# Low parts of the first attention's probabilities folded into idle rows of the outer key chunks

## The chip, the cores and the metric

The kernel runs on one core of one Trainium2 chip. A core has a matrix engine (TensorE, PE in the profile, with its weight loads shown apart as PEld), a vector engine (VectorE, DVE), a scalar engine (ScalarE, ACT), a general engine (GpSimd, POOL) and a queue-only engine (SyncE, SP) that here issues almost all DMA transfers. Each engine runs its instructions in a fixed order. The metric is the time of one execution on the device in microseconds (us); the median of several runs is compared.

## The reference: one encoder layer with two attentions

The reference computes one layer over 2048 tokens of width 1024: a norm, one wide input product, two attentions, a gated merge, and an MLP of width 4096 with a final norm. Only the first attention matters here:

```python
def windowed_gqa(q, k, v, sink):          # q (B,S,8,64); k,v (B,S,2,64)
    ...
    def block(i):                         # 128 queries, 384 keys from (i-1)*128
        ...
        dist = jnp.abs(q_pos[:, None] - k_pos[None, :])
        valid = (dist <= A_WINDOW) & (k_pos[None, :] >= 0) & (k_pos[None, :] < s)
        sc = jnp.einsum('bqkgd,bskd->bkgqs', qi, ki).astype(jnp.float32) * scale
        sc = sc - slopes[:, :, None, None] * dist.astype(jnp.float32)
        sc = jnp.where(valid, sc, -jnp.inf)
        ...
        p = jax.nn.softmax(jnp.concatenate([sc, sink_col], axis=-1), axis=-1)[..., :-1]
        return jnp.einsum('bkgqs,bskd->bqkgd', p.astype(v.dtype), vi)
```

There are 16 blocks of 128 queries, 2 key/value groups of 4 query heads each, head size 64, and a window of 128 tokens to each side (A_WINDOW). All of it is float32.

## The kernel before: one attention unit and what runs around it

Products keep float32 accuracy by splitting each operand in a rounded high part and the low rest. [...] Helpers `split` (L296, L297) and `mm3`/`mm3s` (L203 to L205, L300 to L302) do this all over the kernel.

The first attention is cut into 32 units, `attn_a(g, i)`: group g, query block i. Its first half (up to `yield`, L798) loads the queries with four transfers into `q` (L774, tag "qa", 3 buffers) and makes the scores. The 128 queries of 4 heads are regrouped in four sub-blocks u of 32 queries by 4 heads, so a sub-block fills 128 rows. Sub-block u looks at 288 keys only, from 32u to 32u+288 of the 384 that belong to the block (L780). Two matmuls make the scores of a sub-block (L785), DVE adds the bias and takes the maximum (L787), ACT takes the exponentials (L789 to L792), DVE sums and inverts (L793, L794), POOL scales (L796). The tile `s` (tag "sa") is 128 rows by 4 sub-blocks by 384 keys, and its columns outside the 288 keys were zeroed once (L754) and stay zero.

Its second half multiplies the probabilities by v. For each chunk c of 128 keys (three of them; the first block has no chunk 0, the last no chunk 2, so there are 92 chunks in all, and 60 of them are outer ones, c = 0 or 2), PE turns four 128x128 pieces into `pt` (L803): 128 keys in the rows, 512 columns in the order (u, head, query). ACT rounds `pt` to the high part `ph` (L806), DVE subtracts to get the low part `pl` (L807), and PE multiplies both by the same weights, v's 128 rows for this chunk with the high parts of v in columns 0 to 63 and the low parts in columns 64 to 127 (L808 for `ph`, L809 for `pl`). ACT and DVE add the two halves of the result `po` (L814, L815) and a transfer stores it (`y_a`, issued at L176).

In an outer chunk many rows of `pt` are zero. In chunk 0, sub-block u starts at key 32u, so for u = 2 and 3 (columns 256 to 511) rows 0 to 63 are zero. In chunk 2, sub-block u ends before row 32(u+1), so for u = 0 and 1 (columns 0 to 255) rows 64 to 127 are zero.

The first halves run two units ahead of the second halves (`drive`, L829). The weights of v come from `va` (L762), which `load_kv` fills per group and per half of the sequence. Between the attention's instructions lie those of the rest of the input product for the last two token blocks ("filler": `qk_tile`, `v_tile`, `gate_tile`, 24 matmuls of 128x512 for one tile, PE lines L203 to L205), which `paced` (L839) ties to the end of earlier units through `issue_after(done[at])`, where `done` holds each unit's last matmul. All loads of queries, keys, v and filler weights and the stores of results are issued by SP in one queue, in order.

The order on each engine, and on SP's queue, is not the order of the code: a planner (`TileContext(nc, schedule_with_timeline_sim=True)`) simulates the program with its own costs and writes down the order that its simulation gives. A tile of a ring with 3 buffers waits, in the plan and by a semaphore on the chip, until the last reader of the tile three back is done. Any change to the instructions may thus change the planned order of others.

Of the kernel before, what the change touches and what calls it, by code (L numbers as in the profile page):

```python
# [8 lines left out]
F32 = mybir.dt.float32  # L9
F32R = mybir.dt.float32r  # L10
AF = mybir.ActivationFunctionType
ALU = mybir.AluOpType
# [10 lines left out]
P = 128  # L23
# [72 lines left out]
def encoder_layer(ctx, tc, x, norm_mix, w_in, b_gate, sink, rpb, w_pa, w_pb, w_out,  # L96
                  norm_mlp, w_up, w_down, norm_final, dist_a, mask_b, out):
    nc = tc.nc
    V, A, G, PE, SY = nc.vector, nc.scalar, nc.gpsimd, nc.tensor, nc.sync

    def pool(name, side=None, space=None, stack=None):
        kw = {"reuse_waits": "tile"} if space is not DRAM else {}
        if side:
            kw["side"] = side
        if space:
            kw["space"] = space
        return (stack or ctx).enter_context(tc.tile_pool(name=name, bufs=1, **kw))

    def pools(stack, side, tags, name):

        return {t: pool(f"{name}_{t}", side=side, stack=stack) for t in tags}
# [9 lines left out]
    def psum(tag, bufs):  # L121
        n_ps[0] += 1
        return pps[tag].tile([P, 512], F32, tag=tag, bufs=bufs, name=f"{tag}_{n_ps[0]}")
# [3 lines left out]
    def T(pl, shape, dt, tag, bufs):  # L127
        n_t[0] += 1
        pl = pl[tag] if isinstance(pl, dict) else pl
        return pl.tile(shape, dt, tag=tag, bufs=bufs, name=f"{tag}_{n_t[0]}")  # L130
# [25 lines left out]
    vs_a = [dp.tile([2, P, 8, P], F32, name=f"vs_a{m}") for m in range(2)]  # L156
# [14 lines left out]
    def put(dst, src):  # L171
        pending.append((dst, src))

    def flush(keep=0, queue=A):
        while len(pending) > keep:
            queue.dma_start(*pending.pop(0))  # L176
# [398 lines left out]
    for p in range(2):  # L575
        t = T(xp, [P, D], F32, "xin", 8).rearrange("p (k c) -> p k c", k=4)
        c = QUADS[2][0]
# [93 lines left out]
    s_h = ExitStack()  # L671
    hpl = [pool(f"hT{n}", side="left", stack=s_h) for n in range(4)]
    s_a = ExitStack()
    ap_ = pools(s_a, "left", ("ka1", "va1", "qa", "sta", "sa", "ya", "dist", "ph", "pl", "biasa1", "byhead"), "a")
    ap_.update(pools(s_a, "right", ("biasa0", "va0", "ka0"), "a"))
    hp = {}

# [49 lines left out]
    dist = T(ap_, [P, A_K], F32, "dist", 1)  # L727
# [5 lines left out]
    for h in range(4):  # L733
        at = slice(h * A_Q, (h + 1) * A_Q)
# [4 lines left out]
    def make_bias_a(g):  # L739
        t = T(ap_, [P, A_K], F32, f"biasa{g}", 1)  # L740
        G.tensor_scalar(t, dist, slope[:, g : g + 1], 1.0, ALU.mult, ALU.mult)
        bias_a[g] = t
# [21 lines left out]
    def attn_a(g, i):  # L764
        c0, c1 = (1 if i == 0 else 0), (2 if i == 15 else 3)
        if bias_a[g] is None:

            with tc.issue_after(shares[2]):
                make_bias_a(g)
        base = (i - 1) * P  # L770
        q = T(ap_, [P, 4, 4, A_Q], F32R, "qa", 3)
        s = sas[len(began) % 4]
        for h in range(4):
            asked = SY.dma_start(q[:, :, h].bitcast(F32), qs_a[g][i // 8][:, h, i % 8].rearrange("p (u q) -> p u q", u=4)).ins  # L774
        began.append(asked)
        ka, v = kas[g], vas[g]
        st = T(ap_, [P, 8, 4], F32, "sta", 8)
        mx, nm, sm, es, ri = (st[:, k, :] for k in range(5))
        sink_g = sink_p[:, g : g + 1]
        span = [(max(u * A_Q, c0 * P), min(u * A_Q + A_K, c1 * P)) for u in range(4)]  # L780
        for u, (lo, hi) in enumerate(span):
            n = hi - lo
            ps = psum("s", 3)
            for z in range(2):
                PE.matmul(ps[:, :n], q[:, u].rearrange("p h q -> p (h q)"), ka[:, z, base + lo : base + hi],  # L785
                          start=z == 0, stop=z == 1)
            V.tensor_tensor_reduce(out=s[:, u, lo:hi], in0=ps[:, :n], in1=bias_a[g][:, lo - u * A_Q : hi - u * A_Q],  # L787
                                   scale=1.0, scalar=sink_g, op0=ALU.add, op1=ALU.max, accum_out=mx[:, u : u + 1])
        A.activation(nm, mx, AF.Copy, scale=-1.0)  # L789
        A.activation(es, mx, AF.Exp, bias=sink_g, scale=-1.0)  # L790
        for u, (lo, hi) in enumerate(span):
            A.activation(s[:, u, lo:hi], s[:, u, lo:hi], AF.Exp, bias=nm[:, u : u + 1], accum_out=sm[:, u : u + 1])  # L792
        V.tensor_tensor(out=sm, in0=sm, in1=es, op=ALU.add)  # L793
        V.reciprocal(ri, sm)  # L794
        for u, (lo, hi) in enumerate(span):
            share = G.tensor_scalar(s[:, u, lo:hi], s[:, u, lo:hi], ri[:, u : u + 1], 1.0, ALU.mult, ALU.mult)  # L796
        shares.append(share.ins)
        yield  # L798
        po = psum("av", 1)
        for c in range(c0, c1):  # L800
            pt = psum("pt", 2)
            for u in range(4):
                PE.transpose(pt[:, u * P : (u + 1) * P], s[:, u, c * P : (c + 1) * P], ident)  # L803
            ph = T(ap_, [P, 512], F32R, "ph", 3)
            pl = T(ap_, [P, 512], F32R, "pl", 3)
            A.copy(ph, pt)  # L806
            V.tensor_tensor(out=pl, in0=pt, in1=ph.bitcast(F32), op=ALU.subtract)  # L807
            PE.matmul(po, v[:, i - 1 + c, :], ph, start=c == c0, stop=False)  # L808
            last = PE.matmul(po, v[:, i - 1 + c, :], pl, start=False, stop=c == c1 - 1).ins  # L809
        done.append(last)  # L810
        t = T(ap_, [64, 512], F32, "ya", 2)
        t4 = t.rearrange("d (h u q) -> d h u q", h=4, u=4)
        by_u = po.rearrange("p (u h q) -> p h u q", u=4, h=4)
        A.copy(t4, by_u[64:128])  # L814
        V.tensor_tensor(out=t4, in0=by_u[0:64], in1=t4, op=ALU.add)  # L815
        flush(queue=SY)
        put(y_a[g].rearrange("(h d) t -> d h t", d=64)[:, :, i * P : (i + 1) * P],
            t.rearrange("d (h q) -> d h q", h=4))
# [56 lines left out]
    for g in (1, 0):  # L875
        load_kv(g, 0)
    drive((attn_a(g, i) for g in (1, 0) for i in range(7)), live, False)
    paced(fill, range(12), 24, 3)
    flush(queue=SY)
    for g in range(2):  # L880
        load_kv(g, 1, began[8 + 3 * g])
    drive((attn_a(g, i) for g in range(2) for i in range(7, 16)), live, True)
    paced(fill, range(12, 24), 24, 3)
    del done[:]
# [700 lines left out]
    for n in (1, 6, 2, 7, 5, 3, 4):  # L1585
        for group in ((range(8),) if n != 4 else (range(4), range(4, 8))):
            part = None if n != 4 else group[0] // 4
# [13 lines left out]
            last = []  # L1601
# [55 lines left out]
```

## Time and profile before

| | us |
|---|---|
| median of 3 runs | 2614.83 (2614.39 to 2615.31) |
| profiled execution | 2611.98 |
| its span, first to last instruction | 2610.2 |
| PE busy in the span | 2573.7 (99%) |
| DVE busy | 1605.5 (62%) |
| ACT busy | 1231.4 (47%) |
| POOL busy | 348.9 (13%) |
| first and last score matmul of the first attention (L785) | 361.7 to 612.0 |
| first and last v matmul of the first attention (L808) | 382.7 to 652.1 |

Durations in the profile overlap: a matmul's own duration is longer than the distance to the start of the next. So the cost of a matmul on PE is read from the distance of the starts in the timeline, and the mean durations of the grouped lines only tell which shapes there are. In a grouped line, after the bar stand the busy time, the mean of one in ns, and then the idle time of the engine before these instructions with what ended it. "SPq" is SP's queue of transfers; "PEld" is the weight load.

### The profile page before, as it was taken

The page shows a single profiled execution, that of the slowest core. Times are in us where ns is not written, and L with a number is a line of the kernel's source. Part 1 is how long each engine was busy: PE and PEld are TensorE (multiplying, and loading weights), DVE is VectorE, ACT ScalarE, POOL GpSimd, SP SyncE. Part 2 cuts the span into 40 slices and gives each one's busy share as a digit, 9 for nine tenths or more (in the row PEclk, how much of TensorE's full clock was granted, in tenths as well). Part 3 has the DMA queues.
Part 4 walks back from the last instruction along what each step waited for, and adds up shares of the span by engine and source line. Part 5 has one row for each costly group of instructions (what it writes and reads, how often), then busy time and mean ns, then how long its engine had stood idle before and what let it go on. Part 6 is the DMA issues. An engine that isn't in the chain of part 4 may idle for free.

```text
span 2610.2 us, 34770 instructions
## 1 busy us (share of the span) xinstructions
PE 2573.7 (99%) x12140; PEld 2145.4 (82%) x12140; DVE 1605.5 (62%) x2621; ACT 1231.4 (47%) x2261; POOL 348.9 (13%) x461
## 2 busy tenths in 40 slices
PE   8999999999999999999999999999999999999999
PEld 6888778878888888888888888888888888888887
DVE  8865656655544444765578777766656535554766
ACT  5334256665555555533335544644444332323454
POOL 1000013334554541000001000100000000000010
PEclk9999999999999999999999999999999999999999
DMA  5657487575876755865565765854428835445555
GB/s 184 204 154 202 136 224 184 123 178 140 241 209 178 199 146 170 293 190 153 166 201 196 244 212 199 309 184 145 156 98 308 297 97 186 145 146 169 186 191 173
DMA packets 404672, 490.27 MB, mean 188 GB/s; under 512 B 95864, under 2 KB 239352, under 8 KB 402320
## 3 DMA queue, kind: packets, MB, share of 16 engines
q1 hardware_dynamic: 397440, 471.00, 59.1%
q10 hardware_dynamic: 7056, 17.04, 1.8%
q8 instruction: 96, 1.57, 0.3%
q14 instruction: 80, 0.66, 0.1%
HBM read 328.49 MB, written 159.45 MB: 187 GB/s over the span
## 4 chain that ended last, share of the span: by engine, by line
PE 90%; DMA 3%; DVE 3%; ACT 1%; issue 1%; SPq 1%; POOL 0%; DVEq 0%; POOLq 0%; ACTq 0%
PE b L300 16%; PE b L301 16%; PE b L302 16%; PE mm L203 5%; PE mm L205 5%; PE mm L204 5%; PE zb L302 3%; PE zb L300 3%; PE zb L301 3%; PE pt L203 2%; PE pt L204 2%; PE pt L205 2%; PE av L988 2%; PE pt L976 2%; PE s L948 2%; PE pt L803 1%
## 5 line engine op out<-in xcount | busy, mean ns | idle before, releaser
L301 PE MATMUL b<-dwh,dah 128*128 128x512 f32 x896 | 348.5, 389 | 0.0
L302 PE MATMUL b<-dwh,dah 128*128 128x512 f32 x896 | 347.6, 389 | 0.0
L300 PE MATMUL b<-dwh,dah 128*128 128x512 f32 x896 | 339.6, 389 | 0.0
L296 ACT CAST dah<-da 128x1024 fp32r<-128x1024 f32 (+1 forms) x128 | 121.0, 946 | 368.1 <-PE b L302 245.4
L297 DVE TENSOR_TENSOR dah<-da,dah 128x1024 fp32r<-128x1024 f32 (+1 forms) x128 | 139.6, 1090 | 222.3 <-ACT dah L296 219.2
L301 PE MATMUL b<-ubh,uwhlb 128*128 128x512 f32 x592 | 230.3, 389 | 0.0
L300 PE MATMUL b<-ubh,uwhlb 128*128 128x512 f32 x592 | 230.2, 389 | 0.0
L302 PE MATMUL b<-ubh,uwhlb 128*128 128x512 f32 x592 | 229.2, 389 | 0.0
L203 PE MATMUL mm<-hT,whl 128*128 128x512 f32 x544 | 218.9, 402 | 0.0
L205 PE MATMUL mm<-hT,whl 128*128 128x512 f32 x544 | 214.8, 395 | 0.0
L204 PE MATMUL mm<-hT,whl 128*128 128x512 f32 x544 | 214.6, 395 | 0.0
L300 PEld LDWEIGHTS b<-dwh,dah 128*128 128x128 f32 x896 | 168.2, 188 | 34.9
L301 PEld LDWEIGHTS b<-dwh,dah 128*128 128x128 f32 x896 | 168.2, 188 | 34.8
L302 PEld LDWEIGHTS b<-dwh,dah 128*128 128x128 f32 x896 | 168.2, 188 | 34.8
L300 PE MATMUL zb<-zh,zwhl 128*128 128x512 f32 x476 | 186.6, 394 | 8.2 <-DVE zc L293 3.2
L301 PE MATMUL zb<-zh,zwhl 128*128 128x512 f32 x476 | 186.5, 392 | 0.0
L302 PE MATMUL zb<-zh,zwhl 128*128 128x512 f32 x476 | 183.6, 392 | 0.3 <-DVE zwhl L297 0.3
L293 DVE TENSOR_TENSOR uc<-b,uc 128x512 f32<-128x512 f32 x160 | 109.2, 689 | 104.2 <-PE b L302 103.2
L1527 POOL TENSOR_TENSOR st<-st,power 128x1 f32<-128x1 f32 x16 | 13.4, 843 | 925.2 <-DVE st L1526 925.2
L300 PEld LDWEIGHTS b<-ubh,uwhlb 128*128 128x128 f32 x592 | 111.1, 188 | 23.4 <-issue 0.4
L301 PEld LDWEIGHTS b<-ubh,uwhlb 128*128 128x128 f32 x592 | 111.2, 188 | 23.1
L302 PEld LDWEIGHTS b<-ubh,uwhlb 128*128 128x128 f32 x592 | 111.1, 188 | 23.1
(253 smaller groups left out, 5820.6 us busy)
## 6 DMA issues: line engine op xcount, KB each, us to landing
at<-uc SPq DMA_DIRECT2D x224, 256.0 KB
da<-at SPq DMA_DIRECT2D x96, 512.0 KB
dw<-in_w_down_dram SPq DMA_DIRECT2D x160, 256.0 KB
uraw<-in_w_up_dram SPq DMA_DIRECT2D x32, 1024.0 KB
raw<-in_w_in_dram SPq DMA_DIRECT2D x34, 512.0 KB
zraw<-in_w_in_dram SPq DMA_DIRECT2D x16, 1024.0 KB
z<-zg SPq DMA_DIRECT2D x64, 256.0 KB
qa<-qs_a SPq DMA_DIRECT2D x128, 64.0 KB
```

Of the source, the lines that this page charges most:

```text
L203: PE.matmul(ps, lh, rh, start=first, stop=False)
L204: PE.matmul(ps, lh, rl, start=False, stop=False)
L205: PE.matmul(ps, ll, rh, start=False, stop=last)
L293: return eng.tensor_tensor(out=out, in0=a, in1=b, op=op).ins
L296: A.copy(hi, src)
L297: return eng.tensor_tensor(out=lo, in0=src, in1=hi.bitcast(F32), op=ALU.subtract).ins
L300: PE.matmul(ps, lh, rh, start=first, stop=False, skip_group_check=True)
L301: PE.matmul(ps, lh, rl, start=False, stop=False, skip_group_check=True)
L302: PE.matmul(ps, ll, rh, start=False, stop=last, skip_group_check=True)
L948: PE.matmul(ps[:, :n], q[:, i, :], kv[:, z, B_R0[i] // 4 : (B_R0[i] + B_NR[i]) // 4, 4 * B_C0[j] : 4 * (B_C0[j] + w)], start=z == 0, stop= ...
L976: PE.transpose(pt[:kp, at + (i - i0) * P : at + (i - i0 + 1) * P], s[i][:, rr : rr + kp], ident)
L988: last = PE.matmul(po[:, i0 * P : (i0 + ni) * P], v[:kp, c, :], src[:kp, o : o + ni * P], start=first, stop=(c == 7 and z == 1), skip_grou ...
```

## The change

In an outer chunk, the 512 columns are treated as two halves of 256. One half ("full") is done as before: high and low part against v's 128 rows. In the other half ("part"), 64 rows are zero. There, DVE writes the low part of the 64 used rows into the 64 zero rows of the high part's own tile `ph`, and a single matmul multiplies all 128 rows by a second set of weights, `ve`, that holds the 64 v rows which the used rows meet, twice, one copy above the other. Chunk 1 stays as it was.

So an outer chunk has two DVE subtractions of 256 columns (one on 128 rows, one on 64 rows that reads and writes different rows) in place of one of 512, and three matmuls of 256 columns, each with its weight load, in place of two of 512. The doubled v rows are loaded by one more SP transfer of 64 KB for each outer chunk (60 in all), each with a source that repeats the 64 rows twice, into a new tile "ve" of 3 buffers; they are issued in the first half of the unit, after the query loads. A new pool "ve" stands last in the list of the left side's pools.

```diff
-    ap_ = pools(s_a, "left", (..., "biasa1", "byhead"), "a")
+    ap_ = pools(s_a, "left", (..., "biasa1", "byhead", "ve"), "a")
...
         began.append(asked)
+        ve = T(ap_, [P, 2, P], F32R, "ve", 3)
+        for c in range(c0, c1, 2) if c0 == 0 else (2,):
+            src = vs_a[(i - 1 + c) // 8][g][64 - 32 * c : 128 - 32 * c, (i - 1 + c) % 8]
+            (step, _), (one, n) = src.ap
+            SY.dma_start(ve[:, c // 2].bitcast(F32), bass.AP(src.tensor, src.offset, [[0, 2], [step, 64], [one, n]]))
...
             A.copy(ph, pt)
-            V.tensor_tensor(out=pl, in0=pt, in1=ph.bitcast(F32), op=ALU.subtract)
-            PE.matmul(po, v[:, i - 1 + c, :], ph, start=c == c0, stop=False)
-            last = PE.matmul(po, v[:, i - 1 + c, :], pl, start=False, stop=c == c1 - 1).ins
+            vc = v[:, i - 1 + c, :]
+            if c == 1:
+                V.tensor_tensor(out=pl, in0=pt, in1=ph.bitcast(F32), op=ALU.subtract)
+                wide = [(slice(0, 512), vc, ph), (slice(0, 512), vc, pl)]
+            else:
+                full, part = (slice(0, 256), slice(256, 512))[:: 1 - c]
+                kept, other = (slice(64, 128), slice(0, 64))[:: 1 - c]
+                V.tensor_tensor(out=pl[:, full], in0=pt[:, full], in1=ph[:, full].bitcast(F32), op=ALU.subtract)
+                V.tensor_tensor(out=ph[other, part], in0=pt[kept, part], in1=ph[kept, part].bitcast(F32),
+                                op=ALU.subtract)
+                wide = [(full, vc, ph), (full, vc, pl), (part, ve[:, c // 2], ph)]
+            for n, (at, vs, p) in enumerate(wide):
+                last = PE.matmul(po[:, at], vs, p[:, at], start=c == c0 and n == 0,
+                                 stop=c == c1 - 1 and n == len(wide) - 1, skip_group_check=True).ins
```

More of the change, by code (lines that the diff above doesn't have):

```diff
@@ L673, in encoder_layer @@
     s_a = ExitStack()
-    ap_ = pools(s_a, "left", ("ka1", "va1", "qa", "sta", "sa", "ya", "dist", "ph", "pl", "biasa1", "byhead"), "a")
+    ap_ = pools(s_a, "left", ("ka1", "va1", "qa", "sta", "sa", "ya", "dist", "ph", "pl", "biasa1", "byhead", "ve"), "a")
     ap_.update(pools(s_a, "right", ("biasa0", "va0", "ka0"), "a"))
```

## The prediction

> **What bounds the kernel now.** I read the page first, its busy times and the chain that ended last.
>
> ```profile
> span 2610.2 us, 34770 instructions
> ...
> PE 2573.7 (99%) x12140; PEld 2145.4 (82%) x12140; DVE 1605.5 (62%) x2621; ACT 1231.4 (47%) x2261; POOL 348.9 (13%) x461
> ...
> PE 90%; DMA 3%; DVE 3%; ACT 1%; issue 1%; SPq 1%; POOL 0%; DVEq 0%; POOLq 0%; ACTq 0%
> ```
>
> PE is the bound: 99% busy, and 90% of the chain. So PE time that goes away is a gain, unless PE then waits for something. The change lies in the first attention alone, so next come the busy times by stretch, over its whole run and in two short stretches near its start (PE, PEld, DVE, ACT, POOL busy, then the granted clock, the share of the DMA engines, GB/s).
>
> ```profile
> 355.00:655.00 300.00, 290.23 (x1549) 242.32 (x1548) 175.42 (x499) 185.76 (x513) 113.36 (x199) 0.99 0.70 165
> ...
> 388.00:392.00 4.00, 1.94 (x15) 1.64 (x14) 2.32 (x9) 4.00 (x15) 0.00 (x0) 1.00 0.80 180
> 392.00:396.00 4.00, 4.00 (x17) 3.53 (x16) 3.77 (x13) 3.74 (x14) 1.96 (x4) 0.57 1.11 222
> ```
>
> Over the 300 us PE idles 9.8 us (300.00 less 290.23), and no other engine is near full. But at 388 to 392 PE does 1.94 us of work in 4, and in the next stretch its clock is down to 0.57, which costs another 4 x 0.43 = 1.7 us. What ended PE's idle time there, and elsewhere in the attention, stands in the list of waits (engine, line, waited for: total us, times, longest); its last line here is from the same list for SP's queue.
>
> ```profile
> PEld s L785 <- DVE sta L787: 4.2, 7, 1.3
> ...
> PEld av L809 <- DVE pl L807: 3.0, 9, 0.5
> ...
> PE s L785 <- DMA qa<-qs_a: 2.8, 2, 2.1
> ...
> PEld av L808 <- DVE ya L815: 2.5, 5, 1.1
> PEld s L785 <- DVE sta L793: 2.3, 1, 2.3
> PEld pt L803 <- DVE pl L807: 2.3, 1, 2.3
> ...
> SPq L774 <- PE s L785: 42.0, 20, 5.0
> ```
>
> Two causes: DVE is late in 7 + 9 + 5 + 1 + 1 = 23 places, and twice the queries are late.
>
> **PE: the matmuls.** The grouped lines give the shapes that come and go, and the timeline the distances of their starts.
>
> ```profile
> L809 PE MATMUL av<-pl,va 128*128 128x512 f32 x92 | 38.1, 414 | 0.9 <-DVE pl L807 0.4
> L808 PE MATMUL av<-ph,va 128*128 128x512 f32 x92 | 37.9, 412 | 1.6 <-DVE ya L815 1.3
> ...
> L988 PE MATMUL av<-phb,vb 128*128 128x256 f32 x96 | 26.6, 294 | 0.4 <-ACT phb L981 0.2
> ```
>
> ```profile
> 410.20 0.39 PE L808 MATMUL av<-ph,va 128*128 128x512 f32 x1
> 410.42 0.39 PE L809 MATMUL av<-pl,va 128*128 128x512 f32 x1
> 410.66 0.39 PE L808 MATMUL av<-ph,va 128*128 128x512 f32 x1
> 410.89 0.39 PE L809 MATMUL av<-pl,va 128*128 128x512 f32 x1
> ...
> 1002.04 0.28 PE L988 MATMUL av<-phb,vb 128*128 128x256 f32 x1
> 1002.16 0.28 PE L988 MATMUL av<-plb,vb 128*128 128x256 f32 x1
> 1002.28 0.28 PE L988 MATMUL av<-phb,vb 128*128 128x256 f32 x1
> 1002.40 0.28 PE L988 MATMUL av<-plb,vb 128*128 128x256 f32 x1
> ```
>
> From 410.20 to 410.89 three steps of a 512-wide matmul take 0.69 us, 0.23 each. From 1002.04 to 1002.40 three steps of a 256-wide one take 0.36, 0.12 each, with a weight load of its own each time, as in the changed kernel. An outer chunk falls from 2 x 0.23 = 0.46 to 3 x 0.12 = 0.36 us. There are 32 x 3 - 4 = 92 chunks (the x92 above), of which 32 are middle ones, so 60 change: 60 x 0.10 = 6.0 us of PE's time go. It lies on the path, as PE is the bound.
>
> [...]
>
> **DVE: two subtractions for one.** The grouped lines of the subtractions:
>
> ```profile
> L807 DVE TENSOR_TENSOR pl<-pt,ph 128x512 fp32r<-128x512 f32 x92 | 62.4, 686 | 18.6 <-ACT ph L806 18.0
> ...
> L815 DVE TENSOR_TENSOR ya<-av,ya 64x512 f32<-64x512 f32 x32 | 21.8, 680 | 13.9 <-ACT ya L814 13.9
> ...
> L982 DVE TENSOR_TENSOR plb<-pt,phb 128x384 fp32r<-128x384 f32 x32 | 17.2, 553 | 10.8 <-ACT phb L981 10.8
> ```
>
> 64 rows cost as much as 128 (680 and 686 ns), and 128 columns less save 133 ns. So 256 columns cost about 553 - 133 = 420 ns, and two of them 840, 154 ns over the one they replace. Over 60 chunks DVE works 9.2 us more. DVE is busy 175.42 of the 300 us, so most of it lies in its idle time, under PE's filler. It costs PE something only where PE waits for DVE already: 23 places, of which 60 / 92 have an outer chunk before them, so 23 x 0.65 x 0.154 = 2.3 us. The bounds are zero (the planner puts filler before each late matmul) and all 9.2. I take 2.3, nearest to the rows of the waits. What is queued on DVE behind the second subtraction, the bias step of the next unit's scores (L787) and the sum of the halves (L815), is late by the same 0.154 us, and the same 23 places count it.
>
> **The copies of v's rows: 60 more transfers.** SP's queue and the transfers near the start are what they meet: first SP's timeline, then PE's, then the DMA part of the page for 340 to 400 us.
>
> ```profile
> 376.24 2.19 SPq L774 DMA_DIRECT2D qa<-qs_a  x4
> 380.22 0.56 SPq L762 DMA_DIRECT2D va<-vs_a  x1
> ...
> 381.56 3.05 SPq L774 DMA_DIRECT2D qa<-qs_a  x4
> 384.66 2.00 SPq L708 DMA_DIRECT2D ks_a<-z  x3
> 386.76 3.01 SPq L774 DMA_DIRECT2D qa<-qs_a  x4
> ...
> 391.58 0.86 SPq L176 DMA_DIRECT2D y_a<-ya  x1
> ```
>
> ```profile
> 386.43 0.77 PE L785 MATMUL s<-ka,qa 128*128 128x288 f32 x4 [0.79 <-DMA qa<-qs_a]
> ...
> 391.58 0.79 PE L785 MATMUL s<-ka,qa 128*128 128x288 f32 x4 [2.06 <-DMA qa<-qs_a]
> ```
>
> ```profile
> DMA packets 29415, 14.02 MB, mean 234 GB/s; under 512 B 20127, under 2 KB 25954, under 8 KB 29410
> ```
>
> ```profile
> qa<-qs_a SPq DMA_DIRECT2D x36, 64.0 KB
> ```
>
> At 380 to 390 the queue issues without a pause, and PE waits 0.79 and 2.06 us for queries. The first unit's result is stored at 391.58, so until then only the three buffers' first users and the next have their v rows: units 0 to 3, 1 + 2 + 2 + 2 = 7 transfers of 64 KB, 0.45 MB. At 234 GB/s these take 1.9 us, and the queries behind them come so much later. The bounds: zero, where the planner issues them earlier or later, and 7 x 0.56 = 3.9 us of issue (the one row of `va`) plus a second half-clock stretch of 1.7. I take 1.9. After the opening a unit takes about 300 / 32 = 9.4 us, SP waits anyway, and a copy is asked for three units before its use: nothing, covered by that lead. If it is gone, each late copy costs PE what SP lost.
>
> **Waits.** The third matmul of an outer chunk waits for the second subtraction and for its copy. Two waits can need a semaphore instruction more; such a row and the weight loads:
>
> ```profile
> L803 PEldq EVENT_SEMAPHORE  x43: 51/51/51, 371.5 to 638.3; - x43
> ...
> L808 PEld LDWEIGHTS av<-ph,va x92: 186/188/197, 382.6 to 651.9; 128*128 128x128 f32 x92
> ```
>
> 60 x 0.051 = 3.1 us is the upper bound, zero the lower. I take zero: PE's sequencer runs ahead of busy PE, and no idle time above is put down to these 43. ACT and POOL have the same work as before. The ring "ve" lies last in its side's list, so no other tile moves because of it.
>
> **The order.** Any new instruction lets the planner write a new order for the stage. That can take away or add to the 9.8 us of idle time. I take zero, and for the range half of it, 4.9, either way.
>
> **Sum.** -6.0 + 2.3 + 1.9 = -1.8 us. The profiled execution took 2611.98 us (span 2610.2 and 1.8 around it), so it would take 2610.2. It lies 2.85 below the median of the runs, 2614.83; on that scale the forecast is 2613.0.
>
> **Rivals.** *Faster: the costs stay hidden.* DVE is 58% busy in the stage and SP waits often, so both terms can vanish, and 6.0 with some of the idle time gives 2614.83 - 6.0 - 1.5 = about 2607. For it: most places have filler beside them. Against: PE already waits in 23 places for DVE, so the cover is thin there.
>
> *Slower: SP's queue stands still.* The copy for unit n may be written only when unit n - 3 has finished its last v matmul, later than the scores matmul that frees the query buffer. The copy stands in SP's one queue, with the next queries and filler weights behind it. SP's waits for query buffers are 42.0 us over 20, 2.1 each. 36 query transfers in 340 to 400 us are 9 units; the first 3 have free buffers, so 6 wait. If each wait reaches PE, it is 6 x 2.1 = 12.6, and -6.0 + 2.3 + 12.6 = +8.9 us, 2623.7. It decides from (5.2 + 6.0 - 2.3) / 6 = 1.5 us lost by PE per unit. For it: PE's waits of 0.79 and 2.06 us, where the queue is full. Against: the planner places a transfer where its own plan has the buffer free.
>
> *Slower: weight loads become the bound.* If three loads of 0.188 us can't hide behind 256-wide matmuls, a chunk takes 0.56 instead of 0.46, and 60 x 0.10 + 2.3 + 1.9 = +10.2 us, 2625. The steps of 0.12 at 1002 speak against it.
>
> **How the numbers follow.** 0.2% is 5.2 us, about what a measurement of this kernel can tell from no change: within is 2609.6 to 2620.1. The forecast (gain paid back, within) has 0.37, the faster rival 0.30, SP's queue 0.30, the weight loads 0.03; so faster 0.30, same 0.37, slower 0.33. The likeliest case alone spans 2609.6 to 2620. With both sides likely, the range reaches from all costs hidden and half the idle time gone (2614.83 - 6.0 - 4.9 = 2603.9) to DVE, SP, clock and semaphore bounds together (-6.0 + 9.2 + 3.9 + 1.7 + 3.1 = +11.9, 2626.7), with a little of the queue rival's tail: 2604 to 2628.
>
> **What would show it.** After: 32 pairs of 512-wide v matmuls and 180 of 256 at steps of 0.12; two subtractions of about 420 ns; idle PE time over the stage near 9.8 + 4.2 us; SP's waits at the copies short. I am wrong if PE waits for copies or for queries behind them, if the clock falls in further stretches, or if the planned order moves the idle time by more than 5 us.

## The result, and the profile after

The changed kernel takes 2628.21 us (median of 6 runs, 2626.09 to 2629.91); the kernel before takes 2613.80 us beside it (6 runs). The ratio is 1.0058 (1.0049 to 1.0068): slower by 0.58%, some 15 us, and the interval lies clear of 1. The forecast was 2613.0, the range 2604 to 2628. The profiled execution of the change took 2629.91 us, against 2611.98 before.

The page of the changed kernel, its span and busy times:

```profile
span 2628.0 us, 35078 instructions
...
PE 2577.2 (98%) x12200; PEld 2154.6 (82%) x12200; DVE 1619.0 (62%) x2681; ACT 1233.1 (47%) x2261; POOL 348.4 (13%) x461
```

PE's busy time did not fall, although 256-column matmuls took the place of wider ones; the rows below say why. First the busy times by stretch (columns as in the prediction). The stretch shown is now 355 to 675 us, since the last v matmul of the first attention starts at 670.5 and not at 652.8.

```profile
355.00:675.00 320.00, 295.11 (x1618) 250.78 (x1617) 186.57 (x551) 184.70 (x506) 107.65 (x192) 0.97 0.70 167
...
384.00:388.00 4.00, 0.45 (x2) 0.02 (x1) 0.00 (x0) 1.07 (x4) 0.25 (x1) 1.00 0.17 40
388.00:392.00 4.00, 0.16 (x1) 0.19 (x2) 0.00 (x0) 0.00 (x0) 0.00 (x0) 0.62 0.69 126
392.00:396.00 4.00, 4.00 (x18) 3.81 (x19) 1.65 (x8) 0.42 (x1) 2.01 (x5) 0.53 0.96 236
468.00:472.00 4.00, 0.80 (x5) 0.44 (x3) 3.55 (x14) 3.98 (x14) 1.58 (x4) 0.86 0.82 178
472.00:476.00 4.00, 4.00 (x16) 3.81 (x17) 0.34 (x2) 0.64 (x3) 2.31 (x5) 0.50 0.82 208
```

PE idles 24.9 us in the stage (320.00 less 295.11), where it idled 9.8 before: 15.1 more. At 384 to 392 all engines stand almost still. After that, and again at 472, PE works at about half its clock (0.53 and 0.50), so its matmuls last longer (one of 512 columns 0.63 us at 392.94, 0.40 at 398.38) and its busy time does not fall: with the same instructions in the same order and faster copies (the run with the steps exchanged, below) PE is busy 2571.0 us, 6.2 less. At the first fall the clock is 0.50 from about 389 us on, when PE had stood idle for 4.5 us. At the second it is 1.00 up to 470.84 us and 0.50 from 470.90 on, when PE had been idle for 2.1 us, since 468.74.

What PE waited for, from the list of waits (total us, times, longest):

```profile
PE s L790 <- DMA qa<-qs_a: 12.3, 4, 7.4
...
PEld av L824 <- DVE ph L820: 2.3, 9, 0.3
```

The weight loads of the v matmuls wait for the second subtraction (L820) in 9 places, 2.3 us in all; before, they waited 3.0 us in 9 places for the only one. In PE's timeline, the last matmul before the longest wait, and the two longest waits:

```profile
384.06 0.39 PE L205 MATMUL mm<-hT,whl 128*128 128x512 f32 x1
391.84 1.30 PE L790 MATMUL s<-ka,qa 128*128 128x288 f32 x4 [7.40 <-DMA qa<-qs_a]
...
471.89 0.82 PE L790 MATMUL s<-ka,qa 128*128 128x288 f32 x2 [3.15 <-DMA qa<-qs_a]
```

PE waits 12.3 us for queries, 2.8 before: 9.5 of the 15.1 us that it idles more. The other two of the four waits, 1.41 and 0.30 us, end at 578 and 586 us. So 4.9 us of the 12.3 come after the opening of the stage. What stood ahead of the queries is in the timeline of SP's queue:

```profile
376.81 0.46 SPq L761 DMA_DIRECT2D ka<-ks_a  x1
377.31 8.19 SPq L780 DMA_DIRECT2D ve<-vs_a  x5
385.60 4.15 SPq L774 DMA_DIRECT2D qa<-qs_a  x4
...
465.05 1.13 SPq L780 DMA_DIRECT2D ve<-vs_a  x2
466.23 1.46 SPq L774 DMA_DIRECT2D qa<-qs_a  x2
```

At 465 the queries were issued right behind two copies, and PE got them at 471.89, 4.2 us after their last issue ended; in the opening that took 2.1 us. That the copies ahead of them delayed their landing is argued, not shown.

In the opening, five copies of v's rows held SP for 8.19 us. They were not held by busy DMA engines. The DMA part of the page for 383 to 387 us, where only these copies run:

```profile
DMA packets 301, 0.15 MB, mean 38 GB/s; under 512 B 5, under 2 KB 301, under 8 KB 301
...
q1 hardware_dynamic: 301, 0.15, 15.2%
```

The engines are 15.2% busy, which is the time of 16 x 0.152 = 2.4 of them, and they move 38 GB/s. At that rate one copy of 64 KB takes 1.7 us. So 84.8% of the engines' time was idle while the queries waited in SP's queue.

The durations of the new instructions came as forecast. The timeline of PE and the grouped lines of the subtractions:

```profile
443.49 0.28 PE L824 MATMUL av<-pl,va 128*128 128x256 f32 x1
443.61 0.28 PE L824 MATMUL av<-ph,ve 128*128 128x256 f32 x1
443.73 0.40 PE L824 MATMUL av<-ph,va 128*128 128x512 f32 x1
```

```profile
L820 DVE TENSOR_TENSOR ph<-pt,ph 64x256 fp32r<-64x256 f32 x60 | 25.3, 422 | 1.6
L819 DVE TENSOR_TENSOR pl<-pt,ph 128x256 fp32r<-128x256 f32 x60 | 25.3, 422 | 19.5 <-ACT ph L811 19.0
```

A 256-wide matmul takes 0.12 us from start to start, and a half subtraction 422 ns.

### The profile page after: what moved, and what is told of

Same layout as the page of the kernel before. It is cut to its first block, busy times and chain, and to the rows that moved or that the text cites. A ratio compares the mean times of both kernels' runs of the same rounds, so it can differ in the third digit from the quotient of the medians.

```text
span 2628.0 us, 35078 instructions
## 1 busy us (share of the span) xinstructions
PE 2577.2 (98%) x12200; PEld 2154.6 (82%) x12200; DVE 1619.0 (62%) x2681; ACT 1233.1 (47%) x2261; POOL 348.4 (13%) x461
## 4 chain that ended last, share of the span: by engine, by line
PE 91%; DVE 3%; DMA 3%; ACT 1%; issue 1%; SPq 1%; POOL 1%; POOLq 0%; DVEq 0%; ACTq 0%
PE b L300 15%; PE b L301 15%; PE b L302 15%; PE mm L203 6%; PE mm L205 6%; PE mm L204 6%; PE zb L302 3%; PE zb L300 3%; PE zb L301 3%; PE pt L203 2%; PE pt L204 2%; PE pt L205 2%; PE av L1004 2%; PE pt L992 2%; PE s L964 2%; PE av L824 1%
```

## The experiments

A transfer's source is written as a list of pairs of a step and a number, the outermost first: `[[0, 2], [step, 64], [one, n]]` reads 64 rows of n elements, and all of them twice, since the outermost step is 0. The theory formed from these rows: the source of a copy names its 64 rows twice by an outermost number of 2, and this number holds the copy to a few engines (the time of 2.4, by the 15.2% above) and so to 38 GB/s. The rivals: SP's waits for buffers (the prediction's slower case), the mere number of transfers, the second subtraction, and the planner's new order. All ratios are to the kernel before, timed on the same chip (its medians there: 2611.94 for the first four runs, 2612.18 to 2613.85 for the others).

**The same number of transfers, rows not doubled.**

```diff
-            SY.dma_start(ve[:, c // 2].bitcast(F32), bass.AP(src.tensor, src.offset, [[0, 2], [step, 64], [one, n]]))
+            SY.dma_start(ve[:, c // 2].bitcast(F32), vs_a[(i - 1 + c) // 8][g][:, (i - 1 + c) % 8])
```

> Each of the 60 transfers into the tile "ve" reads 128 different rows of v (one step of 128 rows) instead of 64 rows twice (an outer step of 2, an inner one of 64). Number, bytes, packet size, buffers and place in SP's queue stay. The single matmul of the half columns then meets wrong v rows, so that part of the result is not the reference's. Theory (the doubled source makes the transfer run on a few of the 16 DMA engines: about 38 GB/s at 383 to 387 us of the changed kernel, and SP's queue stands behind it): the five first copies land within 2 us, PE's wait for queries in the opening falls from 7.4 us to under 3, and the time is 2608 to 2617. Rival (the queue's waits for free buffers, or 60 more transfers of any kind, cost the time): 2624 to 2632, as with the doubled source.

Measured: 2612.84 us, ratio 1.0002 (0.9993 to 1.0011). The loss is gone with the number of transfers and their bytes unchanged. SP's queue, in the same place as above:

```profile
375.86 3.76 SPq L778 DMA_DIRECT2D ve<-vs_a  x5
379.72 3.17 SPq L774 DMA_DIRECT2D qa<-qs_a  x4
```

The five copies hold the queue 3.76 us and not 8.19. PE's and SP's planned orders differ from the change's in places, so this alone doesn't exclude the planner.

**Two transfers of 64 rows for each copy.**

```diff
+            for z in (0, 64):
+                SY.dma_start(ve[z : z + 64, c // 2].bitcast(F32), src)
```

> The copy is made by two transfers of 64 rows of 512 B each, one to the upper and one to the lower 64 rows of "ve"; 120 transfers in place of 60, the same bytes. Theory (few engines because of the outer step of 2): as fast as with rows not doubled, 2608 to 2618, with up to 2 us for 60 more issues. Rival (number of transfers on SP's queue): slower than the change, 2630 to 2645.

Measured: 2619.77 us, ratio 1.0028 (1.0016 to 1.0040). No number of 2 stands outermost any more, but the ten transfers in the opening hold SP's queue nearly as long as the five of the change did:

```profile
373.91 7.20 SPq L780 DMA_DIRECT2D ve<-vs_a  x10
```

The time lies between the theory's range and the rival's: the number of transfers on this queue has its price too, some 7 us for 60 more (2619.77 less 2612.84).

**No copies at all.**

```diff
-        ve = T(ap_, [P, 2, P], F32R, "ve", 3)
-        ...
-                wide = [(full, vc, ph), (full, vc, pl), (part, ve[:, c // 2], ph)]
+                wide = [(full, vc, ph), (full, vc, pl), (part, vc, ph)]
```

> No tile "ve" and no copies; the matmul of the half columns takes v's own 128 rows as weights, so its part of the result is not the reference's. PE's and DVE's instructions are those of the change. Theory (the copies alone make the change slow): 2607 to 2613, that is the 6.0 us of PE less up to 3 for the second subtraction. Rival (second subtraction or the planner's new order): 2617 to 2628.

Measured: 2608.49 us, ratio 0.9986 (0.9977 to 0.9994), 3.7 us (1.6 to 6.0) faster. Matmuls and subtractions alone are a gain. The copies turn it into the loss.

**The copies alone.** The chunk's compute is that of the kernel before; the loop with the 60 transfers stays.

> The compute of the kernel before, and the 60 doubled copies into "ve" beside it, which nothing reads. Theory (copies on few engines): 2622 to 2636, the loss of the change plus the 6 us of PE that are not saved. Since nothing reads the copies, their buffers come free at once, so the planner can put them earlier than in the change: a larger pile at the start. Rival (waits for buffers that the last v matmul frees): these waits are gone here, so 2613 to 2618.

Measured: 2671.09 us, ratio 1.0222 (1.0208 to 1.0235): the sign is the theory's, the size is far over its 2636. With no reader, a copy's buffer is free at once, and all 60 are issued from 374.7 to 535.1 us, where the change spreads them to 645.9. PE waits for queries 32.0 us in 8 places:

```profile
PE s L790 <- DMA qa<-qs_a: 32.0, 8, 6.9
```

That slow copies cost more the closer they are packed, and that this explains all of the 59 us, is argued, not shown.

**The order of the steps alone.** This is the sharpest run: the planned order on PE, DVE, ACT, POOL and SP is the changed kernel's, instruction by instruction.

```diff
-                         bass.AP(src.tensor, src.offset, [[0, 2], [step, 64], [one, n]])
+                         bass.AP(src.tensor, src.offset, [[step, 64], [0, 2], [one, n]])
```

> The changed kernel with one edit: the two outer steps of the copy's source change places, so each of the 64 rows is read twice in a row (64 outside, 2 inside) instead of all 64 and then all again. The same rows are read as often, in the same number of packets, and the planned order of all engines and of SP's queue is the changed kernel's. The copies lie in "ve" in another order, so the half columns meet wrong v rows. Theory (the size of the outermost step, 2, keeps the transfer on two engines): the five first copies land within 2 us of each other's issue, PE's wait of 7.4 us in the opening falls under 3.5, and the time is 2610 to 2618. Rival A (reading the same rows twice is slow), rival B (the planner's new order): 2625 to 2631, as the change.

Measured: 2611.87 us, ratio 0.9991 (0.9982 to 1.0000). Reading the same rows twice is not slow, and the planner's new order is not the loss: 16 us (2628.21 less 2611.87) hang on which of two numbers stands first. PE's longest wait for queries is 2.1 us, where it was 7.4 (first line: total us, times, longest), and SP's queue is free sooner:

```profile
PE s L790 <- DMA qa<-qs_a: 4.9, 3, 2.1
```

```profile
375.46 3.78 SPq L780 DMA_DIRECT2D ve<-vs_a  x5
379.78 2.02 SPq L774 DMA_DIRECT2D qa<-qs_a  x4
```

**An outermost number of 4.**

```diff
-                         [[0, 2], [step, 64], [one, n]]
+                         [[0, 4], [step, 32], [one, n]]
```

> The changed kernel with the copies' source made of an outer step of 4 and an inner one of 32 (32 rows read four times) in place of 2 and 64; bytes, packets and the planned order of all engines and queues as in the change; the half columns meet wrong v rows. Theory (the outermost number sets the number of engines, so the rate): 76 GB/s where the change has 38, five copies in some 4.3 us in place of 8.6, and a time between: 2612 to 2622. Rival (any copy whose repeats lie outermost is slow): 38 GB/s and 2625 to 2631.

Measured: 2613.10 us, ratio 1.0007 (0.9998 to 1.0015). The stretch 381 to 382 us of this kernel, where the copies run almost alone (the last three figures are PE's clock, the share of the DMA engines and GB/s), and SP's queue:

```profile
381.00:382.00 1.00, 1.00 (x6) 0.84 (x5) 0.93 (x3) 1.00 (x5) 1.00 (x3) 1.00 0.33 87
```

```profile
376.94 3.56 SPq L780 DMA_DIRECT2D ve<-vs_a  x5
380.91 2.66 SPq L774 DMA_DIRECT2D qa<-qs_a  x4
```

The DMA engines are 33% busy, the time of 5.3 of 16, and move 87 GB/s, some of it other transfers. The copies' own packets, of 512 B, are 148 in this microsecond of the trace, 76 GB/s: twice the number, twice the 38 GB/s of the change. So for these copies the rate went with the outermost number, 38 GB/s at 2 and 76 at 4. The time is at the fast end of what was expected. The 2.4 engines of the change are also in its packets: 296 packets of the copies start in 4 us, two every 27 ns, and each lasts about 33 ns, and 2 x 33 / 27 is 2.4. On how many engines the copies ran, and on which, no run shows, so the engines remain the theory's account of the rate; nor is it shown how a source with an outermost 2 that repeats nothing fares.

**An outer step of 2 without doubling.**

```diff
+            SY.dma_start(ve[:, c // 2].bitcast(F32), bass.AP(src.tensor, src.offset, [[64 * step, 2], [step, 64], [one, n]]))
```

> 128 different rows are read (nothing twice), but the source is written with an outer step of 2 and an inner one of 64; the planned order of PE, DVE, ACT and POOL is the changed kernel's. The half columns meet wrong v rows. Theory (an outermost step of 2): as slow as the change, 2624 to 2631, with the same 38 GB/s while the copies run. Rival A (reading the same rows twice is slow): 2610 to 2617.

Measured: 2611.53 us, ratio 0.9989 (0.9980 to 0.9998), against the theory's 2624 to 2631. But two steps that follow on one another without a gap are one step of 128, and so the trace seems to have them: the transfer's shape is 128 by 1 here, as in the run with rows not doubled, and 1 by 128 in the change (and with the steps exchanged, where the copies are quick, so the shape alone does not tell the speed). So it tested something else than meant: the change's compute with fast copies, once more.

**The second subtraction alone.**

```diff
+            for at in (slice(0, 512),) if c == 1 else (slice(0, 256), slice(256, 512)):
+                V.tensor_tensor(out=pl[:, at], in0=pt[:, at], in1=ph[:, at].bitcast(F32), op=ALU.subtract)
```

> The kernel before with the subtraction of outer chunks made in two instructions of 256 columns on 128 rows; PE's matmuls as before, no copies. By the prediction's term: +2.3 us, bounds 0 to +9.2, so 2612 to 2621 where the kernel before takes 2612; each half about 420 ns. If it is over +5 us, the gain of the matmuls must have been larger than 6.0 to give what the run without copies gave.

Measured: 2613.08 us, ratio 0.9995 (0.9986 to 1.0004). By the interval it costs at most 1 us; the 2.3 of the prediction is over that.

**The matmuls alone.**

```diff
+                wide = [(full, vc, ph), (full, vc, pl), (part, vc, ph)]
```

with the one subtraction of 512 columns as before.

> The kernel before with the three matmuls of 256 columns in outer chunks, the half columns' single one with v's own rows and the high part alone (their low part is left out of the result); one subtraction of 512 columns as before, no copies. By the prediction's term: 60 x 0.10 = 6.0 us less, 2606 to 2609 where the kernel before takes 2613; within 1 us of the run without copies if the second subtraction costs nothing, 2 to 3 us under it if that costs the 2.3 us forecast. Rival (weight loads bound the 256-wide matmuls): 2613 or more.

Measured: 2609.82 us, ratio 0.9991 (0.9982 to 1.0000), 2.4 us faster (0 to 4.7), and not 6.0: just over the 2606 to 2609 expected. Its page:

```profile
PE 2567.9 (98%) x12200; PEld 2147.0 (82%) x12200; DVE 1605.5 (62%) x2621; ACT 1231.8 (47%) x2261; POOL 348.0 (13%) x461
```

PE's busy time fell by 2573.7 - 2567.9 = 5.8 us, the forecast 6.0. But the span, 2608.0 us, is only 2.2 under that of before: PE's idle time went from 36.5 to 40.1. Of these 3.6 us, 2.5 lie ahead of 355 us, where both kernels run the same instructions, so they tell nothing of the change; from 355 to 655 us PE idles 9.9 us, 9.8 before. From the first score matmul to the last v matmul the first attention takes 288.6 us (361.9 to 650.5), 291.1 before: 2.5 less, as the medians have it. So the work went, and less than half of it as time. Where the rest went is not shown. One thing seen is a second fall of the clock: at 488 to 492 us PE is busy 1.92 of 4 us, and in the next 4 us its clock is 0.67.

**The copies on ACT's queue.**

```diff
-            SY.dma_start(ve[:, c // 2]...
+            A.dma_start(ve[:, c // 2]...
```

> The change with its 60 doubled copies, the source unchanged (an outer step of 2), issued by ACT's queue in place of SP's. Theory (the loss is SP's queue standing behind the copies, not the traffic): the queries come in time, PE's wait for them falls under 4 us in the stage, and the time is 2611 to 2621, with some of it lost where ACT stands behind its own issues. Rival (the transfers on two engines hold up whatever else runs on these two): 2624 to 2640, with PE's waits for queries as long as in the change.

Measured: 2633.25 us, ratio 1.0081 (1.0067 to 1.0095), slower than the change by some 6 us (the two intervals just touch). The time lies in the rival's range, but not by its cause: PE waits for no queries any more, as the theory had it. Instead ACT stands behind its own copies, and the exponentials with it, and PE waits for the probabilities:

```profile
366.40 13.13 ACTq L780 DMA_DIRECT2D ve<-vs_a  x5
379.58 0.20 ACT L794 ACTIVATE sta<-sta 128x4 f32<-128x4 f32 x1 [19.86 <-DMA ve<-vs_a]
```

```profile
382.81 1.54 PE L808 MATMUL pt<-ident,sa 128*128 128x128 f32 x6 [7.03 <-POOL sa L801]
```

Five issues held ACT for 13.13 us, where they held SP for 8.19, and ACT has its own work to do.

**Right copies with rows outermost.** One transfer fills one half of "ve" for both outer chunks: 64 rows outside, the two chunks inside.

```diff
+        for z in (0, 64):
+            if c1 - c0 == 3 and (i - 1) // 8 == (i + 1) // 8:
+                src = vs_a[i // 8][g][64:128, (i - 1) % 8]
+                (step, _), (one, n) = src.ap
+                SY.dma_start(ve[z : z + 64].bitcast(F32),
+                             bass.AP(src.tensor, src.offset, [[step, 64], [2 * n - 64 * step, 2], [one, n]]))
```

> The copies with 64 rows outermost and right in their places: one transfer fills one half of "ve" for both outer chunks of a unit (64 rows, inside it a step of 2 to the other chunk's rows, 512 B each), so about 66 transfers. The same result as the change. Theory: as with rows outermost, 2610 to 2616, at or just under the kernel before. Rival (64 rows in place of 128 are slower, or two transfers of double size hold the queue longer): 2617 to 2624, as with two halves.

Measured: 2611.90 us, ratio 1.0003 (0.9994 to 1.0012). The whole change, with its intended result, at the time of the kernel before: some 14 us under the change by the ratios, and no gain.

**POOL makes the copies.** Three versions: in the unit's first half, with 3 buffers; in its second half, with 4; and in the first half with 8 buffers, ordered behind the scaling of the unit before.

```diff
+            rows = v[64 - 32 * c : 128 - 32 * c, i - 1 + c, :]
+            for z in (0, 64):
+                G.tensor_copy(out=ve[z : z + 64, c // 2], in_=rows.bitcast(F32))
```

> The change with the copies made by POOL from v's rows that already lie in SBUF: two instructions of 64 rows by 128 columns for each outer chunk (120 in all), no transfers. Theory (the transfers alone spoil the change): near the run without copies, 2607 to 2613 where the kernel before takes 2612. Rival: POOL's 120 instructions at about 0.3 us (36 us of its 187 idle in the stage) come late for the scaling (L801) or the weight splitting (L180), and 2613 to 2622.

> POOL makes the copies, as in the run before, but in the unit's second half and with 4 buffers, so that POOL does not stand waiting for the last v matmul (54.4 us over 17 waits there) ahead of the scaling. The same result as the change. Theory (that wait was the loss): 2608 to 2613, near the run without copies. Rival (35 us more POOL work, or its instructions' effect on other engines): 2614 to 2620 again.

> POOL makes the copies from v in SBUF, with 8 buffers, each unit's copies ordered on POOL behind the scaling of the unit before. The same result as the change. Theory (POOL's wait for free buffers ahead of the scaling was the loss): the wait falls from 54 us to under 15, and 2607 to 2612 where the kernel before takes 2612 to 2614. Rival (35 us of added POOL work on the way to the probabilities): 2613 to 2619.

Measured: 2616.18 us, 1.0012 (1.0004 to 1.0021); 2616.87 us, 1.0017 (1.0009 to 1.0026); 2626.20 us, 1.0056 (1.0044 to 1.0069). The first two lie in the ranges of their rivals, the third over both. In the first, the copies cost POOL 34.7 us, and it stands before them until the last v matmul frees a buffer:

```profile
L781 POOL CAST ve<-va 64x128 fp32r<-64x128 f32 x120 | 34.7, 289 | 65.2 <-PE av L824 54.4 <-PE pt L808 5.8
```

The second kept that wait (56.0 us over 17), so it tested nothing new. The third took it away, and got slower; its longest idle times of PE are waits for queries in the opening (4.9 us) and for the second attention's queries at 665 us (5.4 us). So taking POOL's wait away did not bring the gain. Whether the added work, that wait or the order that came with each version cost the time, stays open.

## Why the prediction was wrong

The step that failed is "The copies of v's rows: 60 more transfers", in the words "at 234 GB/s these take 1.9 us". 234 GB/s is the mean of everything that ran from 340 to 400 us. The copies' source starts with a 2, and they ran at 38 GB/s: not 1.9 us for seven, but 1.7 us for each. All told the copies cost some 19 us of the kernel's time (the ratios of the change and of the run without copies, 1.0058 and 0.9986). Fast copies, as in the run with the steps exchanged (0.9991), come to some 1.3 us, known to some 3, so the 1.9 would have done for those; the rate was what the step had wrong. The upper bound (3.9 us of issue and one more half-clock stretch) rested on the issue of a transfer with 128 rows outermost, 0.56 us, and was as wrong: five issues took 8.19 us.

The same step put the copies at nothing after the opening, "covered by that lead". The lead did cover the copies: PE never waits for one. It did not cover the queries behind them: three waits, 4.9 of the 12.3 us, and a second fall of the clock come later.

The direction of what follows was in the prediction, as the rival "SP's queue stands still": PE late for queries in the opening, 8.9 us slower, 2623.7. Its place was right, its mechanism was not. It had SP waiting for a free buffer; the run with the steps exchanged has the same buffers and the same planned order, and no loss. The clock's fall was among the signs named, and came.

*PE, 6.0 us.* Right as work: 0.12 us a matmul, and 5.8 us of busy time gone in the run of the matmuls alone. As time it was mis-sized: 2.4 us (0 to 4.7) alone. Costing it in full "as PE is the bound" was too much; where the rest went stays open, as PE's idle time in the stage is the same (9.9 and 9.8 us).

*DVE, 2.3 us.* The durations were right (422 ns for 420 forecast), the cost was not: the interval of the run with the second subtraction alone ends at 1 us. That the planner's filler covers it is argued, not shown.

*Sum of these two.* Forecast -3.7 us, measured without copies -3.7 (-6.0 to -1.6). That it fits is luck: both terms were too large, and they have opposite signs. The intervals are as wide as the terms.

*The planner's order, taken as zero.* Not refuted: with the change's order and fast copies the ratio is 0.9991, but no run has the order apart from the rest.

*The weight loads as the bound* did not occur (0.12 us a step). The semaphore waits, taken as zero, were not tried alone.

## What to carry to other kernels

Here a transfer's cost lay in its access pattern and not in its bytes, so look at the outermost number of the source: with a repeat of 2 there the copies ran at 38 GB/s, with the repeat moved inside the kernel took 16 us less, and with each copy split in two of 64 rows 8.4 us less (2628.21 less 2619.77). A slow transfer cost most through its queue here: the queries behind it waited, and ACT, when it issued the copies, stood for 13.13 us. Saved work on a 99% busy engine is not yet saved time: here 2.4 of 6.0 us arrived, by the medians.

## What the runs showed of the hardware that was not expected

- Two orders of the same two steps, with the same bytes and planned order, differ by 16 us in the whole kernel: 38 GB/s for an outermost 2, and 76 for an outermost 4.
- SP's queue stood behind slow transfers while the DMA engines were mostly idle: in the change five issues took 8.19 us, and the DMA engines were 15.2% busy at 383 to 387 us; with an outermost 4 the five took 3.56.
- One idle stretch cost twice: after 7.4 us without work PE ran at a clock of 0.53 over the next 4 us. 2.1 us of idle time stood before the fall to 0.50 at 470.9 us, while in the kernel before 2.9 us of idle time ended at 267.5 us and the clock was 1.00 from 262 to 272 us.
